# One sum per chunk for two parts of the output projections

## The chip, the cores and the metric

The kernel runs on one core of a Trainium2 chip: TensorE (PE) for matmuls, VectorE (DVE), ScalarE (ACT) and GpSimd (POOL) for the elementwise work, and SyncE (SP) for issuing DMAs. The metric is the device time of one execution in microseconds, as the median of some runs.

## What is computed

A decoder trunk of two layers on one sequence of 512 tokens with 1024 channels, in float32. Cut to what matters here:

```
for each layer:
    h = rms_norm(x)
    heads = attention(h @ w_in)        # 16 heads of 64; layer 0: 8 dilated, 8 sliding-window; layer 1: 16 forgetting
    x = x + concat(heads) @ w_out      # the output projection, 1024 x 1024
    h = rms_norm(x)
    x = x + relu(h @ w_up)**2 @ w_down
```

The output projection with its residual, `x + concat(heads) @ w_out`, is what the change is about.

## The kernel before

**Products in three parts.** Every operand of a large matmul is kept as a high half rounded to fp32r and the low half that remains (`split`, `parts`). `mm3` makes three matmuls of 128 x 128 weights and 512 columns: high weights with high data, low with high, high with low. A weight tile is loaded raw (tag `wraw`, 4 buffers, which the residual's tiles `xl` and the MLP's weights share), then split into `whi` and `wlo` (7 buffers each). Which engine does the two halves goes by a table: `PAT_OP` for the output projection.

**Pairs of heads.** Heads are worked in pairs of 64 rows each, eight pairs per layer. `attend` makes a head's scores (`S`, then the reduction `negm`, the exponential, the sum `den` and its reciprocal `rden`), scales the probabilities `P`, transposes them (`PT`) and multiplies them with the values (`O`). While one head's scores are made, the values of the head before run. With a pair's second head `yf` is complete and is split into `y`.

**The output projection.** `out_part(pairs, first, ...)` makes the part of the product that belongs to some pairs: for each of eight chunks of 128 output channels it sums `mm3` over these pairs in one PSUM bank `op` and adds the bank to the accumulator `acc` on VectorE. The first part adds the residual `xl`; the later ones add to what `acc` holds. There are three parts: in layer 0 pairs 0, 1, 4, 5, then 6, 7, and in the end 2, 3; in layer 1 pairs 0 to 3, then 4, 5, and in the end 6, 7. The last part belongs to the MLP's function, which takes up each chunk at once (`finish`), and whose weights `w_up` are loaded ahead.

**What sets the order.** `run` interleaves the attention of the last pairs with the first two parts of the output projection: it takes a step of one or of the other by their shares of the work (`LEADS`). A scheduler then orders each engine's instructions, except those that are kept in program order. PSUM has eight banks here: four (`pA`) for `pj` and `op`, four (`pB`) for the attention's `S`, `PT`, `O` and `qkT`. SP issues its DMAs in order: weights, the residual, and the copies of K to the other half of the partitions (line 313).

Of the kernel before, what the change touches and what calls it, by code (L numbers as in the profile page):

```python
# [9 lines left out]
F32 = mybir.dt.float32  # L10
# [8 lines left out]
P = 128  # L19
# [10 lines left out]
RAW = 4  # L30
# [15 lines left out]
REST = 11  # L46
UNP = True
AHEAD = ()
LD1 = 6
PRE0 = 3  # L50
LS = 2
# [9 lines left out]
LEADS = (0.0, 0.0, -0.16, 0.33, -0.3, -0.23, -0.09)  # L61
# [8 lines left out]
def trunk(ctx, tc, x, b_sinks, w_out_even, b_forget, w_out_odd, w_up, w_down, xt, gains, w_in_even, w_in_odd, out):  # L70
    nc = tc.nc
# [5 lines left out]
    wp = ctx.enter_context(tc.tile_pool(name="wp", bufs=3))  # L77
# [3 lines left out]
    def bank(tag, name):  # L81
        return ps.tile([P, 512], F32, tag=tag, bufs=BANKS[tag], name=name)
# [4 lines left out]
    def acc_slot(name):  # L87
        return act.tile([P, 2, 512], F32, tag="acc", bufs=4, name=name)
# [74 lines left out]
    def mm3(o, wh, wl, xh, xl, start, stop, pin=False, more=False):  # L163

        m = nc.tensor.matmul(o, wh, xh, start=start, stop=False, skip_group_check=more)  # L165
        if pin:
            tc.keep_in_program_order(m)
        nc.tensor.matmul(o, wl, xh, start=False, stop=False, skip_group_check=more)  # L168
        nc.tensor.matmul(o, wh, xl, start=False, stop=stop, skip_group_check=more)  # L169
# [23 lines left out]
    def residual(li, dp):  # L193

        return xsp[dp] if li else xt[dp * 256:(dp + 1) * 256].rearrange("(c p) t -> p c t", p=P)

    def layer_attention(li, hT, w_in, w_out, stats=None):


        with ExitStack() as c2:  # L200
# [211 lines left out]
            ys = [None] * 8  # L412
# [31 lines left out]
            def last_values():  # L444
                for _ in head_values(last_head[0]):
                    yield
                last_head[0] = None

            def chain(*gens):
                for g in gens:  # L450
                    yield from g

            def run(att, n_att, dense, n_dense, lead=0.0):

                a = d = 0
                while True:
                    if d / n_dense <= (a + lead * n_att) / n_att or att is None:
                        c = next(dense, None)
                        if c is None:
                            break  # L460
                        d += c
                    else:
                        if next(att, "end") == "end":
                            att = None
                        a += 1
                if att is not None:
                    for _ in att:
                        pass

            accs = []  # L470

            def out_weights(pairs, c0):

                np_ = len(pairs)
                w = 1024 // np_
                runs, k = [], 0
                while k < np_:
                    m = k
                    while m + 1 < np_ and pairs[m + 1] == pairs[m] + 1:
                        m += 1  # L480
                    runs.append((k, 0, w_out[pairs[k] * P:(pairs[m] + 1) * P, c0 * P:c0 * P + w]))
                    k = m + 1
                return load_w(runs, w, np_, PAT_OP)

            def out_part(pairs, first, finish=None, tiles=None):

                np_ = len(pairs)
                w = 1024 // np_
                tiles = tiles or {}
                for c in range(DC):  # L490
                    c0, e = c // (w // P) * (w // P), c % (w // P)
                    if c0 not in tiles:
                        tiles[c0] = out_weights(pairs, c0)
                    ws = tiles[c0]
                    cw = slice(e * P, (e + 1) * P)
                    if first and c % 2 == 0:
                        xl = wp.tile([P, 2, 512], F32, tag="wraw", bufs=RAW, name="xl")
                        nc.sync.dma_start(xl, residual(li, c // 2))
                        accs.append(acc_slot(f"acc{li}_{c // 2}"))
                    o = bank("pA", "op")  # L500
                    for kk, n in enumerate(pairs):
                        mm3(o, ws[kk][0][:, cw], ws[kk][1][:, cw], ys[n][:, 0], ys[n][:, 1], kk == 0, kk == np_ - 1)
                    a = accs[c // 2][:, c % 2]
                    nc.vector.tensor_add(a, o, xl[:, c % 2] if first else a)
                    if finish is not None:
                        finish(c, a)
                    yield 32 * np_

            tiles = {}

            def ahead(pairs):
                for c0 in AHEAD:
                    tiles[c0] = out_weights(pairs, c0)
                    yield 0
# [18 lines left out]
            def all_of(gen):  # L533
                for _ in gen:
                    pass

            if li == 0:
                def qk_a(g):
                    return project([(g * 768, g * 768 + 512)], qk_use(g, 8))

                def v_a(g):
                    return project([(g * 768 + 512, g * 768 + 768)], v_use(g, 0), PAT_START if g == 0 else PAT_ATT)

                def att_a(g):
                    def get(p_):
                        qk = st["qk", g]
                        return prep_q(qk, p_ * P), prep_k(qk, 256 + p_ * P, gg[:, 0:1])
                    return attend(get, 256, lambda: st["v", g], lambda j: j, "a", 4 * g, 2, 2 * g)

                def kv_b():  # L550
                    def use(outs):
                        st["v", 3] = prep_v(outs, P, 2, 1)
                        st["k", "b"] = norm_heads(outs, 2)
                    return project([(2048, 2304)], use, PAT_START)

                def att_b():
                    def get(p_):
                        if p_ == 0:
                            st["kb"] = prep_k(st["k", "b"], 0, gg[:, 1:2])
                        k = st["kb"][p_ // 2]  # L560
                        return prep_q(st["qk", "b"], p_ * P), [k, k]
                    return attend(get, 0, lambda: st["v", 3], lambda j: j // 4, "b", 0, 4, 4)

                start(ap, hT, w_in, make_tables(ap, dist, lt, lb), [bank("pA", f"pj{t}") for t in range(NT)], qk_use(0, 8, "P3", 2))
                all_of(v_a(0))
                run(att_a(0), 32, chain(kv_b(), project([(1536, 2048)], qk_use("b", 8))), 768, LEADS[0])
                run(att_b(), NB, chain(qk_a(1), v_a(1)), 768, LEADS[1])
                run(chain(att_a(1), last_values()), 38, chain(out_part([0, 1, 4, 5], True),
                                                              out_part([6, 7], False), ahead([2, 3])), 1536, LEADS[2])
                last = [2, 3]  # L570
            else:
                def qk_c(g):
                    return project([(g * 768, g * 768 + 512)], qk_use(g, 8))

                def v_c(g):
                    return project([(g * 768 + 512, g * 768 + 768)], v_use(g, g))

                def vf_c():
                    def use(outs):
                        forget(ap, outs)  # L580
                        v_use(0, 0)(outs)
                    return project([(512, 768), (3072, 3088)], use, PAT_START)

                def att_c(g):
                    def get(p_):
                        qk = st["qk", g]
                        return prep_q(qk, p_ * P), prep_k(qk, 256 + p_ * P, gg[:, 2:3])
                    return attend(get, 256, lambda: st["v", g], lambda j: j, "c", 4 * g, 2, 2 * g)

                g = vf_c()  # L590
                for _ in range(STATS):
                    next(g)
                stats()
                all_of(g)
                all_of(qk_c(0))
                for g in range(3):
                    run(att_c(g), 36, chain(qk_c(g + 1), v_c(g + 1)), 768, LEADS[3 + g])
                run(chain(att_c(3), last_values()), 42, chain(out_part([0, 1, 2, 3], True),
                                                              out_part([4, 5], False), ahead([6, 7])), 1536, LEADS[6])
                last = [6, 7]  # L600

            def finish(f):
                all_of(out_part(last, False, f, tiles))

            return accs, finish

# [635 lines left out]
    accs, end = layer_attention(0, [], w_in_even[0], w_out_even[0])  # L1242
    hT, stats = mlp(0, accs, end, False)
    accs, end = layer_attention(1, hT, w_in_odd[0], w_out_odd[0], stats)
# [39 lines left out]
```

## Time and profile before

| | us |
|---|---|
| median of 3 runs | 1161.94 |
| lowest, highest | 1161.77, 1162.87 |
| the profiled execution | 1160.99 |
| its span | 1159.2 |

The granted TensorE clock is 1.00 of full speed over the whole span. PE is the matmul engine and PEld its weight loads, which overlap the matmuls. In a timeline a matmul's end is modelled, and matmuls overlap each other; a distance of two starts says when the engine took the next. Rows of one line and shape that follow each other are put together, with their count behind. What stands in brackets is the idle time ahead of an instruction and what ended it. An instruction that waits holds up all that stands behind it on its engine or queue.

### The profile page before, as it was taken

The page shows a single profiled execution, that of the slowest core. Times are in us where ns is not written, and L with a number is a line of the kernel's source. Part 1 is how long each engine was busy: PE and PEld are TensorE (multiplying, and loading weights), DVE is VectorE, ACT ScalarE, POOL GpSimd, SP SyncE. Part 2 cuts the span into 40 slices and gives each one's busy share as a digit, 9 for nine tenths or more (in the row PEclk, how much of TensorE's full clock was granted, in tenths as well). Part 3 has the DMA queues.
Part 4 walks back from the last instruction along what each step waited for, and adds up shares of the span by engine and source line. Part 5 has one row for each costly group of instructions (what it writes and reads, how often), then busy time and mean ns, then how long its engine had stood idle before and what let it go on. Part 6 is the DMA issues. An engine that isn't in the chain of part 4 may idle for free.

```text
span 1159.2 us, 17365 instructions
## 1 busy us (share of the span) xinstructions
PE 1141.9 (99%) x6228; PEld 977.8 (84%) x6228; DVE 873.0 (75%) x1865; ACT 645.2 (56%) x1342; POOL 198.1 (17%) x292
## 2 busy tenths in 40 slices
PE   9999999999999999999999999999999999999998
PEld 7887887888989988988988888888888888888887
DVE  7878899969868857855647877778858759669676
ACT  7555867655545455444335685655756455465452
POOL 0445434100000000000255545332100000000000
PEclk9999999999999999999999999999999999999999
DMA  8432114232333332433443433343420722523403
GB/s 288 131 91 74 55 38 146 75 108 91 93 108 92 112 105 76 123 96 111 147 128 109 110 101 98 111 129 117 161 86 18 230 80 67 188 73 111 147 34 109
DMA packets 94695, 126.57 MB, mean 109 GB/s; under 512 B 5888, under 2 KB 66304, under 8 KB 94608
## 3 DMA queue, kind: packets, MB, share of 16 engines
q1 hardware_dynamic: 93568, 123.29, 34.7%
q10 hardware_dynamic: 1040, 2.16, 0.5%
q8 instruction: 49, 0.80, 0.3%
q14 instruction: 38, 0.31, 0.1%
HBM read 114.39 MB, written 4.23 MB: 102 GB/s over the span
## 4 chain that ended last, share of the span: by engine, by line
PE 84%; DVE 8%; DMA 3%; ACT 2%; issue 2%; POOL 1%; SPq 0%; POOLq 0%; DVEq 0%; ACTq 0%
PE up L165 10%; PE up L169 10%; PE up L168 10%; PE pj L236 4%; PE pj L234 4%; PE pj L235 4%; PE O L405 3%; PE PT L385 2%; PE op L169 2%; PE op L165 2%; PE op L168 2%; PE Y L1045 2%; PE Y L1042 2%; PE Y L1044 2%; PE Y L1091 1%
## 5 line engine op out<-in xcount | busy, mean ns | idle before, releaser
L165 PE MATMUL up<-xin,whi 128*128 128x512 f32 x512 | 200.6, 392 | 0.0
L169 PE MATMUL up<-xin,whi 128*128 128x512 f32 x512 | 199.4, 389 | 0.0
L168 PE MATMUL up<-xin,wlo 128*128 128x512 f32 x512 | 199.3, 389 | 0.0
L791 ACT CAST whi<-wraw 128x512 fp32r<-128x512 f32 x228 | 139.2, 619 | 105.1 <-PE up L169 47.7
L792 DVE TENSOR_TENSOR wlo<-wraw,whi 128x512 fp32r<-128x512 f32 x228 | 151.6, 685 | 50.9 <-ACT whi L791 50.7
L169 PEld LDWEIGHTS up<-xin,whi 128*128 128x128 f32 x512 | 96.1, 188 | 20.1
L168 PEld LDWEIGHTS up<-xin,wlo 128*128 128x128 f32 x512 | 96.2, 188 | 19.9 <-issue 0.2
L165 PEld LDWEIGHTS up<-xin,whi 128*128 128x128 f32 x512 | 96.2, 188 | 19.6 <-issue 0.2
L365 ACT ACTIVATE P<-P,negm 128x128 f32<-128x128 f32 (+5 forms) x128 | 69.5, 543 | 42.7 <-DVE negm L362 40.3
L973 ACT ACTIVATE u<-up 128x512 f32<-128x512 f32 x64 | 38.3, 598 | 90.9 <-PE up L169 90.9
L234 PE MATMUL pj<-whi,hn 128*128 128x512 f32 (+2 forms) x256 | 88.7, 347 | 0.0
L236 PE MATMUL pj<-whi,hn 128*128 128x512 f32 (+2 forms) x256 | 87.0, 340 | 0.0
L235 PE MATMUL pj<-wlo,hn 128*128 128x512 f32 (+2 forms) x256 | 86.9, 339 | 0.0
L153 POOL TENSOR_SCALAR whi<-wraw 128x512 fp32r<-128x512 f32 x88 | 59.7, 680 | 158.7 <-PE pj L236 137.6
L812 DVE TENSOR_TENSOR t<-u 128x256 f32<-128x256 f32 x56 | 23.2, 423 | 62.8 <-ACT u L1116 61.1
L156 POOL TENSOR_TENSOR wlo<-wraw,whi 128x512 fp32r<-128x512 f32 x48 | 63.8, 1332 | 21.4 <-ACT whi L151 18.9
L156 DVE TENSOR_TENSOR wlo<-wraw,whi 128x512 fp32r<-128x512 f32 (+1 forms) x71 | 49.0, 698 | 18.6 <-POOL whi L153 15.1
L373 POOL TENSOR_SCALAR P<-P,rden 128x256 f32<-128x256 f32 (+2 forms) x96 | 48.0, 503 | 82.8 <-DVE rden L368 77.2
L397 ACT CAST PT<-PT 128x256 fp32r<-128x256 f32 (+3 forms) x128 | 48.9, 403 | 20.3 <-PE PT L385 19.4
L362 DVE CUSTOM_DVE_ANT_0 P<-S,bias 128x128 f32<-128x128 f32 (+1 forms) x96 | 45.7, 484 | 17.4 <-PE S L351 11.8
L791 ACT CAST whi<-mraw 128x512 fp32r<-128x512 f32 x64 | 38.8, 620 | 33.1 <-DVE mraw L902 14.4
L385 PE MATMUL PT<-ident,P 128*128 128x128 f32 x296 | 53.4, 276 | 2.4 <-DVE negm L362 1.4
(241 smaller groups left out, 3083.5 us busy)
## 6 DMA issues: line engine op xcount, KB each, us to landing
wraw<-in_w_up SPq DMA_DIRECT2D x64, 512.0 KB, 4.3
wraw<-in_w_down SPq DMA_DIRECT2D x56, 512.0 KB, 3.8
wraw<-in_w_in_odd SPq DMA_DIRECT2D x22, 512.0 KB, 3.8
wraw<-in_w_in_even SPq DMA_DIRECT2D x17, 512.0 KB, 5.0
mraw<-in_w_down SPq DMA_DIRECT2D x16, 512.0 KB, 4.7
K<-K SPq DMA_DIRECT2D x26, 256.0 KB, 2.9
bias<-csp SPq DMA_DIRECT2D x16, 256.0 KB, 3.3
wraw<-in_w_out_odd SPq DMA_DIRECT2D x8, 512.0 KB, 3.7
```

The costliest lines, as they stand in the source:

```text
L153: nc.gpsimd.tensor_scalar(dst_h, src, 1.0, 1.0, op0=OP.mult, op1=OP.mult)
L156: in_order((nc.gpsimd if lo == "pool" else nc.vector).tensor_sub(dst_l, src, dst_h.bitcast(F32)))
L165: m = nc.tensor.matmul(o, wh, xh, start=start, stop=False, skip_group_check=more)
L168: nc.tensor.matmul(o, wl, xh, start=False, stop=False, skip_group_check=more)
L169: nc.tensor.matmul(o, wh, xl, start=False, stop=stop, skip_group_check=more)
L234: nc.tensor.matmul(o, xh, hi[:, :n], start=k == 0, stop=False)
L235: nc.tensor.matmul(o, xh, lo[:, :n], start=False, stop=False)
L236: nc.tensor.matmul(o, xl, hi[:, :n], start=False, stop=k == DC - 1)
L365: nc.scalar.activation(p[:, :ne], p[:, :ne], AF.Exp, scale=-1.0, bias=negm[:, i:i + 1], accum_out=den[:, i:i + 1])
L385: nc.tensor.transpose(pt[:, (i - c) * P:(i - c + 1) * P], pr[i][:, kb * P:(kb + 1) * P], ident)
L791: sca(nc.scalar.copy(dst_h, src))
L792: late.append(lambda: vec(nc.vector.tensor_sub(dst_l, src, dst_h.bitcast(F32))))
```

## The change

Of the three parts of an output projection the first two become one: `out_two(pa, pb)` takes for each chunk a bank, sums the four pairs `pa` into it, leaves it open, sums the two pairs `pb` into it later, and adds the bank and the residual to the accumulator once. `OUT_ORDER` is the order of these steps: "a" and "b" with a chunk's number for the two products, "x" for the load of the residual of two chunks. The sums over `pa` of the first four chunks are made ahead of the first product with `pb`, so that up to four chunks are open in the four banks of `pA`. `out_last` is what is left of `out_part`, for the last part. The number of matmuls is the same; of the adds on VectorE eight per layer are gone.

```diff
--- before.py
+++ after.py
@@ -46,6 +46,8 @@
 REST = 11
 UNP = True
 AHEAD = ()
+OUT_ORDER = (("a", 0), ("a", 1), ("a", 2), ("x", 0), ("a", 3), ("b", 0), ("x", 2), ("b", 1), ("b", 2), ("b", 3), ("a", 4),
+             ("x", 4), ("b", 4), ("a", 5), ("b", 5), ("a", 6), ("x", 6), ("b", 6), ("a", 7), ("b", 7))
 LD1 = 6
 PRE0 = 3
 LS = 2
@@ -482,28 +484,53 @@
                     k = m + 1
                 return load_w(runs, w, np_, PAT_OP)
 
-            def out_part(pairs, first, finish=None, tiles=None):
+            def out_two(pa, pb):
+
+
+                ws, xls, os = {}, {}, {}
+
+                def product(c, pairs, start, stop):
+                    w = 1024 // len(pairs)
+                    c0 = c // (w // P) * (w // P)
+                    if (len(pairs), c0) not in ws:
+                        ws[len(pairs), c0] = out_weights(pairs, c0)
+                    cw = slice((c - c0) * P, (c - c0 + 1) * P)
+                    for kk, n in enumerate(pairs):
+                        hi, lo = ws[len(pairs), c0][kk]
+                        mm3(os[c], hi[:, cw], lo[:, cw], ys[n][:, 0], ys[n][:, 1], start and kk == 0,
+                            stop and kk == len(pairs) - 1)
+
+                for what, c in OUT_ORDER:
+                    if what == "x":
+                        xls[c // 2] = wp.tile([P, 2, 512], F32, tag="wraw", bufs=RAW, name="xl")
+                        nc.sync.dma_start(xls[c // 2], residual(li, c // 2))
+                        accs.append(acc_slot(f"acc{li}_{c // 2}"))
+                        continue
+                    if what == "a":
+                        os[c] = bank("pA", "op")
+                        product(c, pa, True, False)
+                        yield 32 * len(pa)
+                    else:
+                        product(c, pb, False, True)
+                        nc.vector.tensor_add(accs[c // 2][:, c % 2], os[c], xls[c // 2][:, c % 2])
+                        yield 32 * len(pb)
+
+            def out_last(pairs, finish, tiles):
 
                 np_ = len(pairs)
                 w = 1024 // np_
-                tiles = tiles or {}
                 for c in range(DC):
                     c0, e = c // (w // P) * (w // P), c % (w // P)
                     if c0 not in tiles:
                         tiles[c0] = out_weights(pairs, c0)
                     ws = tiles[c0]
                     cw = slice(e * P, (e + 1) * P)
-                    if first and c % 2 == 0:
-                        xl = wp.tile([P, 2, 512], F32, tag="wraw", bufs=RAW, name="xl")
-                        nc.sync.dma_start(xl, residual(li, c // 2))
-                        accs.append(acc_slot(f"acc{li}_{c // 2}"))
                     o = bank("pA", "op")
                     for kk, n in enumerate(pairs):
                         mm3(o, ws[kk][0][:, cw], ws[kk][1][:, cw], ys[n][:, 0], ys[n][:, 1], kk == 0, kk == np_ - 1)
                     a = accs[c // 2][:, c % 2]
-                    nc.vector.tensor_add(a, o, xl[:, c % 2] if first else a)
-                    if finish is not None:
-                        finish(c, a)
+                    nc.vector.tensor_add(a, o, a)
+                    finish(c, a)
                     yield 32 * np_
 
             tiles = {}
@@ -565,8 +592,7 @@
                 all_of(v_a(0))
                 run(att_a(0), 32, chain(kv_b(), project([(1536, 2048)], qk_use("b", 8))), 768, LEADS[0])
                 run(att_b(), NB, chain(qk_a(1), v_a(1)), 768, LEADS[1])
-                run(chain(att_a(1), last_values()), 38, chain(out_part([0, 1, 4, 5], True),
-                                                              out_part([6, 7], False), ahead([2, 3])), 1536, LEADS[2])
+                run(chain(att_a(1), last_values()), 38, chain(out_two([0, 1, 4, 5], [6, 7]), ahead([2, 3])), 1536, LEADS[2])
                 last = [2, 3]
             else:
                 def qk_c(g):
@@ -595,12 +621,11 @@
                 all_of(qk_c(0))
                 for g in range(3):
                     run(att_c(g), 36, chain(qk_c(g + 1), v_c(g + 1)), 768, LEADS[3 + g])
-                run(chain(att_c(3), last_values()), 42, chain(out_part([0, 1, 2, 3], True),
-                                                              out_part([4, 5], False), ahead([6, 7])), 1536, LEADS[6])
+                run(chain(att_c(3), last_values()), 42, chain(out_two([0, 1, 2, 3], [4, 5]), ahead([6, 7])), 1536, LEADS[6])
                 last = [6, 7]
 
             def finish(f):
-                all_of(out_part(last, False, f, tiles))
+                all_of(out_last(last, f, tiles))
 
             return accs, finish
```

Three places at which the instructions stand differently follow. The lines of the changed file are some two higher than before (362 is 364, 156 is 158).

VectorE in layer 0, from the Q and K of the last pair to its first head's first reduction (`ISA P`, which gives `negm`); before:

```order
L161 SCALAR_TENSOR_TENSOR K_2457<-qkT_2452,gg_85,K_2457 64x512
L301 TENSOR_TENSOR Q_2447<-qkT_2442,Q_2447 64x512
L329 SCALAR_TENSOR_TENSOR bias_2597<-dist_100,lt_101 128x512
L161 SCALAR_TENSOR_TENSOR K_2461<-qkT_2452,gg_85,K_2461 64x512
L504 TENSOR_TENSOR acc0_2_2427<-op_2487,xl_2425 128x512
L156 TENSOR_TENSOR wlo_2629<-wraw_2626,whi_2628 128x512
L156 TENSOR_TENSOR wlo_2633<-wraw_2626,whi_2632 128x512
L504 TENSOR_TENSOR acc0_3_2545<-op_2546,xl_2543 128x512
L362 ISA P_2474,negm_2468<-S_2471,bias_2466 128x128
```

and after:

```order
L331 SCALAR_TENSOR_TENSOR bias_2591<-dist_100,lt_101 128x512
L303 TENSOR_TENSOR Q_2429<-qkT_2424,Q_2429 64x512
L163 SCALAR_TENSOR_TENSOR K_2439<-qkT_2434,gg_85,K_2439 64x512
L303 TENSOR_TENSOR Q_2429<-qkT_2424,Q_2429 64x512
L515 TENSOR_TENSOR acc0_0_2373<-op_2279,xl_2371 128x512
L163 SCALAR_TENSOR_TENSOR K_2443<-qkT_2434,gg_85,K_2443 64x512
L515 TENSOR_TENSOR acc0_1_2463<-op_2324,xl_2461 128x512
L515 TENSOR_TENSOR acc0_1_2463<-op_2374,xl_2461 128x512
L364 ISA P_2456,negm_2450<-S_2453,bias_2448 128x128
```

The two low parts `wlo` no longer stand ahead of the reduction; adds of three chunks do, where there were two.

GpSimd in layer 0, at the scaling of one head's probabilities (line 373, after: 375; from 170 us on in the trace); before:

```order
L373 TENSOR_SCALAR P_2194<-P_2194,rden_2190 128x128
L373 TENSOR_SCALAR P_2202<-P_2202,rden_2190 128x256
L153 TENSOR_SCALAR whi_2539<-wraw_2532 128x512
L373 TENSOR_SCALAR P_2216<-P_2216,rden_2190 128x384
L373 TENSOR_SCALAR P_2308<-P_2308,rden_2304 128x128
L156 TENSOR_TENSOR wlo_2536<-wraw_2532,whi_2535 128x512
L373 TENSOR_SCALAR P_2316<-P_2316,rden_2304 128x256
L156 TENSOR_TENSOR wlo_2540<-wraw_2532,whi_2539 128x512
```

and after:

```order
L155 TENSOR_SCALAR whi_2532<-wraw_2525 128x512
L158 TENSOR_TENSOR wlo_2529<-wraw_2525,whi_2528 128x512
L158 TENSOR_TENSOR wlo_2533<-wraw_2525,whi_2532 128x512
L375 TENSOR_SCALAR P_2194<-P_2194,rden_2190 128x128
L375 TENSOR_SCALAR P_2202<-P_2202,rden_2190 128x256
L375 TENSOR_SCALAR P_2216<-P_2216,rden_2190 128x384
L155 TENSOR_SCALAR whi_2573<-wraw_2571 128x512
L155 TENSOR_SCALAR whi_2577<-wraw_2571 128x512
```

The splits (`whi` on line 153, `wlo` on 156) stood between the scalings of a head; now a high half and two low ones stand ahead of them, and the next splits behind.

ScalarE in layer 0, from the exponential of the last head but one to the transposes of the last (`whi` on line 791, after: 816, are casts of `w_up`); before:

```order
L365 ACTIVATE P_2527,den_2469<-P_2527,negm_2468 128x512
L791 CAST whi_2802<-wraw_2798 128x512
L370 ACTIVATE P_2527<-P_2527,rden_2470 128x512
L408 COPY yf_2185<-O_2569 64x512
L791 CAST whi_2805<-wraw_2799 128x512
L791 CAST whi_2808<-wraw_2798 128x512
L151 CAST y0_2_2594<-yf_2185 128x512
L397 CAST PT_2623<-PT_2618 128x512
L365 ACTIVATE P_2605,den_2600<-P_2605,negm_2599 128x128
L365 ACTIVATE P_2613,den_2600<-P_2613,negm_2599 128x256
```

and after:

```order
L367 ACTIVATE P_2519,den_2451<-P_2519,negm_2450 128x512
L372 ACTIVATE P_2519<-P_2519,rden_2452 128x512
L410 COPY yf_2185<-O_2557 64x512
L816 CAST whi_2786<-wraw_2782 128x512
L153 CAST y0_2_2588<-yf_2185 128x512
L367 ACTIVATE P_2599,den_2594<-P_2599,negm_2593 128x128
L816 CAST whi_2789<-wraw_2783 128x512
L816 CAST whi_2792<-wraw_2782 128x512
L399 CAST PT_2630<-PT_2625 128x512
L367 ACTIVATE P_2620,den_2594<-P_2620,negm_2593 128x256
L399 CAST PT_2652<-PT_2648 128x384
```

The casts of w_up stood one by one and two ahead of the last head; now one stands ahead of y0_2's cast, and two between the exponentials of the last head, ahead of its first transposed tile.

## Rows read from the trace of the kernel before

**Rows 1.** The page, busy time, share of the span and instructions of each engine.
```profile
PE 1141.9 (99%) x6228; PEld 977.8 (84%) x6228; DVE 873.0 (75%) x1865; ACT 645.2 (56%) x1342; POOL 198.1 (17%) x292
```

**Rows 2.** Windows: us, busy of PE, PEld, DVE, ACT, POOL, PEclk, DMA, GB/s.
```profile
150.00:216.00 66.00, 62.20 (x349) 52.32 (x348) 59.83 (x155) 41.10 (x106) 25.69 (x36) 1.00 0.33 96
216.00:300.00 84.00, 84.00 (x449) 72.54 (x448) 69.86 (x130) 51.67 (x94) 0.64 (x1) 1.00 0.31 95
745.00:826.00 81.00, 80.79 (x463) 68.51 (x462) 67.61 (x160) 48.71 (x109) 26.22 (x34) 1.00 0.42 133
```

**Rows 3.** Groups by form: line, engine, operation, shapes, count; busy, mean ns; idle before.
```profile
L792 DVE TENSOR_TENSOR wlo<-wraw,whi 128x512 fp32r<-128x512 f32 x228 | 151.6, 685 | 50.9 <-ACT whi L791 50.7
...
L791 ACT CAST whi<-wraw 128x512 fp32r<-128x512 f32 x228 | 139.2, 619 | 105.1 <-PE up L169 47.7 <-PE Y L1095 14.1 <-DVE wlo L792 8.1
...
L504 DVE TENSOR_TENSOR acc<-op,acc 128x512 f32<-128x512 f32 x32 | 21.7, 682 | 2.9 <-PE op L169 2.6
...
L370 ACT ACTIVATE P<-P,rden 128x512 f32<-128x512 f32 x24 | 17.4, 724 | 4.5 <-DVE rden L368 4.4
```

**Rows 4.** TensorE's timeline: start us, us, engine, line, work, count, idle before.
```profile
155.21 0.40 PE L168 MATMUL op<-y,wlo 128*128 128x512 f32 x1
156.84 0.39 PE L348 MATMUL S<-K,Q 128*128 128x256 f32 x1 [1.23 <-DVE yf L409]
...
173.04 0.38 PE L385 MATMUL PT<-ident,P 128*128 128x128 f32 x2
174.27 0.33 PE L385 MATMUL PT<-ident,P 128*128 128x128 f32 x1 [0.85 <-POOL P L373]
...
186.89 0.39 PE L168 MATMUL op<-y,wlo 128*128 128x512 f32 x1
187.12 0.39 PE L169 MATMUL op<-y,whi 128*128 128x512 f32 x1
...
188.61 0.40 PE L165 MATMUL op<-y,whi 128*128 128x512 f32 x1
190.41 0.55 PE L385 MATMUL PT<-ident,P 128*128 128x128 f32 x3 [1.41 <-DVE negm L362]
...
213.89 0.63 PE L168 MATMUL op<-y,wlo 128*128 128x512 f32 x2
214.83 0.74 PE L169 MATMUL op<-y,whi 128*128 128x512 f32 x2 [0.32 <-DVE y L156]
...
763.62 0.39 PE L168 MATMUL op<-y,wlo 128*128 128x512 f32 x1
764.11 0.36 PE L348 MATMUL S<-K,Q 128*128 128x256 f32 x1
...
812.70 0.39 PE L169 MATMUL op<-y,whi 128*128 128x512 f32 x1
```

**Rows 5.** VectorE's timeline in both output stages.
```profile
153.26 2.81 DVE L275 TENSOR_TENSOR qk<-qk,rs 128x512 f32<-128x512 f32 x2
...
187.43 2.12 DVE L156 TENSOR_TENSOR wlo<-wraw,whi 128x512 fp32r<-128x512 f32 x2
...
213.48 1.30 DVE L156 TENSOR_TENSOR y<-yf,y 128x512 fp32r<-128x512 f32 x1
...
811.46 0.69 DVE L156 TENSOR_TENSOR y<-yf,y 128x512 fp32r<-128x512 f32 x1
```

**Rows 6.** GpSimd's timeline in layer 0's output stage.
```profile
170.08 0.37 POOL L373 TENSOR_SCALAR P<-P,rden 128x128 f32<-128x128 f32 x1 [9.23 <-DVE rden L368]
...
172.53 1.13 POOL L153 TENSOR_SCALAR whi<-wraw 128x512 fp32r<-128x512 f32 x1 [1.35 <-DMA wraw<-in_w_out_even]
173.63 0.93 POOL L373 TENSOR_SCALAR P<-P,rden 128x384 f32<-128x384 f32 x2
...
212.93 1.30 POOL L156 TENSOR_TENSOR wlo<-wraw,whi 128x512 fp32r<-128x512 f32 x1 [8.62 <-ACT whi L151]
```

**Rows 7.** SP's timeline of DMA issues in layer 0's output stage.
```profile
184.01 3.30 SPq L313 DMA_DIRECT2D K<-K  x2
```

## The prediction

> **What bounds the kernel now.** I read the page first. TensorE is busy for 1141.9 us of the span, 99%, VectorE for 75% [rows 1]. Then I cut out the stretches that the change touches: the two output stages (about 155 to 222 us in layer 0, 758 to 822 us in layer 1) and what follows the first [rows 2]. The reader is to see three things there. In layer 0's stage TensorE is busy 62.20 of 66.00 us, so only 3.8 us stand idle; in layer 1's 80.79 of 81.00. Behind layer 0's stage it is busy 84.00 of 84.00, so time gained in the stage isn't lost in the next one, whose work starts as soon as it is its turn. And VectorE is busy 59.83 of 66.00 us, so a wait of TensorE is likely one for VectorE.
>
> So the bound is TensorE's own stream of matmuls, in its program order, and a change that leaves their number as it is can only win or add idle time. The next view is TensorE's timeline around each gap [rows 4]. A 512-column output matmul is shown 0.39 long, but the next one starts 0.23 later (186.89 and 187.12), so a stall costs the distance of two starts less 0.23, which is some 0.16 more than the idle column says:
> at 155: 155.21 to 156.84, 1.63 - 0.23 = 1.40;
> at 173: the idle 0.85 and the 0.16, 1.01;
> at 189: 188.61 to 190.41, 1.80 - 0.23 = 1.57;
> at 214: two matmuls from 213.89, the next at 214.83, 0.94 - 0.46 = 0.48;
> in layer 1, at 764: 763.62 to 764.11, 0.49 - 0.23 = 0.26.
> That is 4.46 us in layer 0 and 0.26 in layer 1. Nothing that reorders these stages can win more than 4.72 us there.
>
> **The change part by part.** It takes eight adds per layer off VectorE, those that add a second part to the accumulator. Here 32 adds of this form take 682 ns each [rows 3], of which 16 go: 16 x 0.682 = 10.9 us of VectorE. The matmuls stay, 3 per chunk and pair. As TensorE is the bound, the 10.9 us count only where they stand before something that TensorE waits for. The loads of weights and of the residual change places as well, and so do the splits.
>
> The stall at 155 comes from VectorE's two normalising multiplications, 2.81 us from 153.26 [rows 5], ahead of the output stage. Nothing is changed ahead of it: 0.
>
> The stall at 173 is a wait for a probability tile that GpSimd scales (the releaser named is the scaling on POOL) [rows 4]. GpSimd had stood idle for 9.23 us before 170.08, then waited at a weight split for its DMA, 1.35, and ran it for 1.13, with the scaling queued behind it [rows 6]. In the new order (second list of the change) this split and two low parts stand ahead of the first scaling, in the idle stretch, and the three scalings follow each other. So this wait goes, if the load lands in the idle stretch. What is late next: the four transposes of the first block of keys now stand in a row, and the fourth needs the tile that ScalarE scales, 0.72 [rows 3]; before, matmuls stood in between. Bounds: all of it (-1.01), none (0). I take -0.45, about the middle, as the fourth tile was 0.72 of ScalarE behind the third.
>
> The stall at 189 is the largest. TensorE waited for the reduction of the next head's scores (negm), which on VectorE stood behind a pair of low parts of weights, 2.12 us from 187.43 [rows 5], and two adds (first list of the change). In the new order two adds stand there and no split, and 28 rather than 24 output matmuls stand on TensorE between the transposes of Q and K and the scores: 4 x 0.23 = 0.9 us more cover. 2.12 + 0.9 = 3.0 against 1.57, so it is gone with 1.4 to spare: -1.57. (If the splits come to stand at another place of the same chain, it stays: 0.)
>
> The stall at 214 is the wait for the low half of the last y, on VectorE 1.30 us from 213.48 [rows 5]. After, 16 output matmuls instead of 13 lie between the last O and its reader (+0.69 of cover), but the add of the last chunk stands ahead of yf's add, and it waits for a product whose end is three matmuls behind O. Worked through, y's low half ends 0.1 to 0.7 later: -0.5 to +0.1. I take -0.2.
>
> In layer 1 the 0.26 is a wait for a K (the second head's). There 24 matmuls stand ahead of the scores instead of 23: -0.23 (0 to -0.26).
>
> Layer 1's end has no stall now: y's low half took 0.69 from 811.46 [rows 5], to 812.15, and its first reader started at 812.70 [rows 4]. In the new order 13 matmuls stand ahead of this reader instead of 15: it comes 0.46 earlier, at 812.24. The last chunk's add now stands right ahead of y's low half, in place of one that ran under ScalarE's cast, and GpSimd's low part of the next weights begins at about the same time. In layer 0 such a pair (212.93 on POOL [rows 6], 213.48 on VectorE) shows 1.30 for the subtraction instead of 0.69. So y's low half ends between 812.3 and 812.9: a stall of 0.1 to 0.7. I take +0.4.
>
> The SP queue: the loads of the second part's weights (two 512 KB tiles) and a residual now stand ahead of the copy of K that was issued at 184.01 [rows 7]. They wait for tiles that GpSimd's and VectorE's splits release; these now come earlier (above), and I read some 3 us of slack, so 0. If they came late, K's copy and the scores behind it would be late by the same.
>
> Sum: 0 - 0.45 - 1.57 - 0.2 - 0.23 + 0.4 = -2.05 us. The profiled execution took 1160.99 us with a span of 1159.2, so 1.8 lie around the span; it would be 1158.9. The median of the runs is 0.95 higher, 1161.94, and would be **1159.9**. The bounds of the terms are -3.84 (1158.1) and +0.8 (1162.7).
>
> **The rivals.** What a measurement of this kernel can tell from no change is about 0.2%, 2.3 us: faster is below 1159.6, slower above 1164.3.
>
> Rival A: every stall but the first goes and no new one comes: 1.01 + 1.57 + 0.48 + 0.26 = 3.3, 1158.6. For it: three of four are waits behind VectorE or GpSimd, which get freer. Against it: the last chunk's add on the way to the last y.
>
> Rival A2: VectorE is the bound in layer 0's stage. It is busy 59.83 of 66.00 us (91%), and 8 x 0.682 = 5.5 us of it go. Then the stage gives back all that TensorE idles, 4.5: 1157.4. Against it: the first stall lies ahead of all that is moved, and from 186.89 output matmuls start every 0.23 with nothing between them. The Trainium skill (Perfetto Trace Analysis, Identifying the Most-Contended Engine) says that matmul busy time is a bad measure, matmuls being pipelined, and that the busy share of weight loads is the good one. By that rule the trace would read 52.32 of 66.00, 79%, for TensorE [rows 2], and VectorE, with 91%, would be the most contended engine of the stage; the starts 0.23 apart in [rows 4] speak for a full TensorE, and I go by them.
>
> Rival C: the stalls move and do not go. In place of the 1.57 TensorE waits as long for a split that now stands elsewhere in the chain: 0 in sum, 1161.9.
>
> Rival B, slower: the MLP's first splits are drawn together. ScalarE's casts and VectorE's low parts of w_up (0.619 and 0.685 each [rows 3]) waited for weight tiles that were released chunk by chunk; now two casts stand together, released by the first part's matmuls of chunk 5 (counted from 0), on ScalarE ahead of the casts and exponentials of the last head's blocks (third list of the change). If chunk 5's matmuls end after those are due, the last head's chain is late by up to 2 x 0.619 + 2 x 0.685 = 2.6 us per layer. It decides from the point at which the cast's release comes behind the first exponential of the last head; matmuls of the next chunk cover a part. With both layers: +5.2, less -0.45 - 1.57 - 0.23 = -2.25, about +2.9: 1164.9. With one layer: about 1162.3, which is no change.
>
> **How the numbers follow.** The forecast -2.05 gets 0.42, with a third of it (0.13) below 1159.6; rival A 0.20, A2 0.08, C 0.14, B 0.16. Faster: 0.13 + 0.20 + 0.08 = 0.41. Same: 0.29 + 0.14 = 0.43. Slower: 0.16. The range: it has to hold 0.80; forecast, A and C and half of A2 do: from 1157.4 (A2) to 1163.6 (C, with the bounds +0.8 of the terms and half of what B adds in one layer). Left out are B and half of A2.
>
> **What the profile after would show.** Right: in layer 0's stage no wait of TensorE of over a microsecond for negm, the PT transposes at 173 with about half the idle time, and the first stall as it is. Busy time of VectorE falls by about 10.9 us in all, and TensorE's stays at 1142. In layer 1's end a wait of up to 0.7 for y's low half. Wrong: TensorE waiting in the last head's stretch for ScalarE or VectorE (B), a wait of 1 to 2 us for K at the scores (the SP queue), or a wait for weights (wlo, whi) at the head of a chunk, which none of the rows before shows.

## The result, and the profile after

The changed kernel took 1163.73 us (median of 20 runs, 1163.06 to 1165.47) against 1161.73 for the kernel before (20 runs, 1160.95 to 1163.25): 1.0018 of the time, with a 95% interval of 1.0012 to 1.0025. That is 2.0 us slower: small, but clear of noise, on the other side of the forecast (1159.9) and 0.1 us outside the range. The profiled execution took 1163.06 us with a span of 1161.3.

The busy times of the page answer to [rows 1]:

```profile
PE 1143.7 (98%) x6228; PEld 977.4 (84%) x6228; DVE 866.2 (75%) x1849; ACT 644.7 (56%) x1342; POOL 199.1 (17%) x292
```

VectorE's busy time fell by 6.8 us (873.0 to 866.2), not by the 10.9 of the sixteen adds. Some of what is left takes longer (the bias operations 0.85 us in all, the splits of `y` 0.9); and busy time counts overlapping records once, as those of operations that run back to back are (1.28 for two of 0.69): taken one by one, the operations' times fell by 9.5. The windows of the two output stages answer to [rows 2] (us, then busy of PE, PEld, DVE, ACT and POOL, PEclk, DMA share, GB/s):

```profile
150.00:216.00 66.00, 63.63 (x352) 52.61 (x350) 55.24 (x149) 41.23 (x106) 25.96 (x36) 1.00 0.33 96
...
745.00:826.00 81.00, 79.61 (x458) 67.00 (x457) 63.11 (x148) 46.83 (x106) 27.24 (x34) 1.00 0.43 134
```

In layer 0's stage TensorE stands idle for 2.4 us and no longer 3.8. In layer 1's it was 0.2 and is now 1.4. VectorE is 4.6 and 4.5 us less busy in the two windows, and only one of them got better by it.

The waits of TensorE in both stages, from its timeline (start us, us, engine, line, work, count, the idle time ahead and what ended it); they answer to [rows 4]:

```profile
157.05 0.38 PE L350 MATMUL S<-K,Q 128*128 128x256 f32 x1 [1.24 <-DVE yf L411]
...
169.02 0.33 PE L351 MATMUL S<-K,Q 128*128 128x384 f32 x1
169.81 0.44 PE L387 MATMUL PT<-ident,P 128*128 128x128 f32 x2 [0.46 <-DVE negm L364]
...
188.84 0.47 PE L350 MATMUL S<-K,Q 128*128 128x512 f32 x1
...
210.20 0.39 PE L170 MATMUL op<-y,wlo 128*128 128x512 f32 x1
210.78 0.51 PE L407 MATMUL O<-PT,v 128*128 128x256 f32 x2 [0.19 <-DVE PT L400]
...
215.13 0.40 PE L167 MATMUL op<-y,whi 128*128 128x512 f32 x1
216.12 0.50 PE L171 MATMUL op<-y,whi 128*128 128x512 f32 x1 [0.60 <-DVE y L158]
...
785.63 0.39 PE L171 MATMUL op<-y,whi 128*128 128x512 f32 x1
...
787.08 0.36 PE L350 MATMUL S<-K,Q 128*128 128x256 f32 x1 [1.07 <-DVE acc L515]
...
814.20 0.63 PE L170 MATMUL op<-y,wlo 128*128 128x512 f32 x2
815.08 0.74 PE L171 MATMUL op<-y,whi 128*128 128x512 f32 x2 [0.26 <-DVE y L158]
```

The first wait, 1.24 at 157, is as it was. The one at 173 is gone, and one for negm stands at 169.81. The largest, 1.41 at 190, is gone: the scores behind it start at 188.84 with no idle time (190.76 before). New are a wait of O for PT at 210.78, a longer one for the last y at 216.12 (215.13 to 216.12, 0.99 less 0.23 is 0.76; 0.48 before), one of 1.22 at 787.08 (785.63 to 787.08, 1.45 less 0.23) and one at 815.08 (0.88 less 0.46 is 0.42).

A ledger puts the two traces side by side. At the same matmul of the attention I took its start, less the start of the stage's first output matmul, less 0.228 us for each output matmul issued by then; the table has after minus before. Both programs have the same attention work between, so a step in this column is time lost or won there.

| up to | output matmuls before, after | after minus before, us |
|---|---|---|
| layer 0: scores at 169.57, after 170.16 | 39, 37 | +0.83 |
| scores at 174.35, after 174.28 | 44, 42 | +0.17 |
| scores at 190.76, after 188.84 | 85, 82 | -1.46 |
| next head's scores, 195.51, after 193.23 | 96, 90 | -1.13 |
| last scores, 199.79, after 198.84 | 108, 108 | -1.17 |
| first w_up matmul, 224.30, after 224.21 | 192, 192 | -0.31 |
| layer 1: scores at 764.11, after 764.44 | 23, 24 | -0.23 |
| scores at 775.91, after 775.97 | 48, 48 | -0.27 |
| last pair's scores, 786.96, after 787.08 | 83, 78 | +0.93 |
| last scores, 798.71, after 800.17 | 108, 108 | +1.13 |
| first w_up matmul, 822.45, after 824.51 | 192, 192 | +1.73 |

So the stage of layer 0, first output matmul to first w_up matmul, went from 69.33 to 69.02 us, and that of layer 1 from 63.92 to 65.65: +1.4 in sum. The other 0.6 of the two profiles' 2.1 lies outside the stages (0.2 ahead of the first, 0.4 between the two, part of it a K that landed 0.2 later at 642 us). The order there is the same, and the ten profiles of this case differ by more at these places whatever the kernel: the first output matmul starts between 154.86 and 156.02 us, and from one stage to the next it takes between 534.05 and 534.96. So I take it as scatter.

### The profile page after: what moved, and what is told of

Its sections match the earlier page's. It is cut to its first block, busy times and chain, and to the rows that moved or that the text cites. A ratio compares the mean times of both kernels' runs of the same rounds, so it can differ in the third digit from the quotient of the medians.

```text
span 1161.3 us, 17348 instructions
## 1 busy us (share of the span) xinstructions
PE 1143.7 (98%) x6228; PEld 977.4 (84%) x6228; DVE 866.2 (75%) x1849; ACT 644.7 (56%) x1342; POOL 199.1 (17%) x292
## 4 chain that ended last, share of the span: by engine, by line
PE 85%; DVE 7%; DMA 2%; ACT 2%; issue 2%; POOL 1%; SPq 0%; POOLq 0%; ACTq 0%; DVEq 0%
PE up L167 10%; PE up L171 10%; PE up L170 10%; PE pj L238 4%; PE pj L236 4%; PE pj L237 4%; PE O L407 3%; PE PT L387 2%; PE op L171 2%; PE Y L1070 2%; PE Y L1067 2%; PE Y L1069 2%; PE op L170 2%; PE op L167 2%; PE S L350 2%
## 5 line engine op out<-in xcount | busy, mean ns | idle before, releaser
L236 PE MATMUL pj<-whi,h 128*128 128x256 f32 (+1 forms) x160 | 54.2, 339 | 1.3 <-DVE v L163 0.9
```

Source lines behind the costliest of these rows:

```text
L236: nc.tensor.matmul(o, xh, hi[:, :n], start=k == 0, stop=False)
```

## The experiments

The theory after the first look: in layer 1 the attention's chain to the last pair's K does not come earlier when O comes earlier, since ScalarE stands in between. The rows of ScalarE and of SP in layer 1 of the changed kernel:

```profile
780.61 0.62 ACT L153 CAST whi<-wraw 128x512 fp32r<-128x512 f32 x1 [1.37 <-DMA wraw<-in_w_out_odd]
781.25 0.58 ACT L410 COPY yf<-O 64x512 f32<-64x512 f32 x1
```

```profile
776.85 0.38 SPq L186 DMA_DIRECT2D wraw<-in_w_out_odd  x1
...
784.07 0.47 SPq L315 DMA_DIRECT2D K<-K  x1
```

and ScalarE's in the kernel before:

```profile
780.52 0.62 ACT L151 CAST whi<-wraw 128x512 fp32r<-128x512 f32 x1 [1.14 <-DMA wraw<-in_w_out_odd]
781.16 0.58 ACT L408 COPY yf<-O 64x512 f32<-64x512 f32 x1
```

O's eight matmuls began at 778.22 (779.52 before) and ended by 779.7, but the copy of O into yf stands behind a cast of a weight tile, whose load was issued at 776.85; the cast waited 1.37 us for it and began at 780.61. Before, it began at 780.52 and O was itself 1.3 us later, so it held yf's copy back by little. So yf, Q and K, and K's copy on SP (784.07; 783.98 before), are where they were, and fewer output matmuls lie ahead of the scores: 54 up to the last pair's transposes, where there were 60, and 78 up to the scores, where there were 83 (the table). 5 x 0.23 = 1.15 us, which is the new wait of 1.22 but for 0.1. The bracket at 787.08 names an add of VectorE, but the scores read K. Of the two copies of K from 780 to 788 us (the view of the tile K) the first landed 2.9 us after its issue, at 786.95, and the scores began 0.13 later, as they did before (landed at 786.82, begun at 786.96):

```profile
DMA to landing us min/median/max: 2.9/3.7/4.6
```

The order of steps explains the 54: `run` takes a step of the output projection as long as its share lags; before, all these steps had twelve matmuls, and the fifth brought it to 60; now after four steps of twelve a step of six already satisfies the share.

**Which layer.** One layer at a time has the change.

```diff
- run(chain(att_c(3), last_values()), 42, chain(out_two([0, 1, 2, 3], [4, 5]), ...
+ run(chain(att_c(3), last_values()), 42, chain(out_part([0, 1, 2, 3], True), out_part([4, 5], False), ...
```

> Layer 0 has the one sum per chunk, layer 1 the parts of before. Theory 1 (the loss lies in layer 1, at the second pair's K): by the two traces layer 0's stage, first output matmul to first w_up matmul, goes from 69.33 to 69.02 us, so this kernel is within 0.3% of the one before, -0.3 us, and its layer 1 stage takes 63.9 us again. Theory 2 (the loss is spread, as later loads of w_up delay the MLP): about half of the +2.0 us, +1.0 us, is left here.

> Layer 1 has the one sum per chunk, layer 0 the parts of before. Theory 1: the whole loss, +1.7 us against before; the layer 1 stage 65.6 us instead of 63.9, with a wait of about 1.2 us at the scores of the last pair and 0.4 at the last y. Theory 2: +1.0 us.

Layer 0 alone: 1161.21 us against 1161.31 (1162.86 for layer 1 alone in the same session), ratio 0.9999 (0.9991 to 1.0008). Layer 1 alone: 1.0014 (1.0005 to 1.0022), +1.6 us. Layer 0's stage is 69.08 us in the first and layer 1's 65.19 in the second, with a wait at the same place, 0.81 us long (1.04 less 0.23) where it was 1.22:

```profile
786.50 0.39 PE L171 MATMUL op<-y,whi 128*128 128x512 f32 x1
787.54 0.35 PE L350 MATMUL S<-K,Q 128*128 128x256 f32 x1 [0.66 <-DVE acc L515]
```

The loss lies in layer 1, theory 1; it is not spread. In this second kernel layer 0, with the parts of before, took 69.03 us and not 69.33: its wait at 190 was 1.25 and not 1.57. So layer 0's -0.31 is no more than the scatter of such a stage.

**More matmuls ahead of the last pair.** One number of the lead is changed.

```diff
-LEADS = (0.0, 0.0, -0.16, 0.33, -0.3, -0.23, -0.09)
+LEADS = (0.0, 0.0, -0.16, 0.33, -0.3, -0.23, -0.07)
```

> The changed kernel with the lead of layer 1's output stage at -0.07 instead of -0.09: one more second-part product (six matmuls) is put ahead of the transposes of the last pair, 60 output matmuls as before the change and not 54. Theory 1 (TensorE runs out of output matmuls while the attention chain waits elsewhere): the wait of 1.2 us at the scores goes, the stage falls to 64.4 us, -1.2 us against the changed kernel. Theory 3 (the K copy itself is late, behind the residual's load on SP): the wait stays at 1.2 us, and the time is that of the changed kernel, +2.0 us against before.

1164.59 us, ratio 1.0027 (1.0016 to 1.0037): slower still, by about 1 us against the changed kernel. The expectation failed as to the time. TensorE's waits in layer 1 (start us, us, engine, line, work, idle before), and ScalarE's row ahead of the second:

```profile
788.39 0.36 PE L350 MATMUL S<-K,Q 128*128 128x256 f32 x1 [0.34 <-DMA K<-K]
...
794.13 0.44 PE L407 MATMUL O<-PT,v 128*128 128x384 f32 x1 [0.59 <-ACT PT L399]
795.02 0.57 PE L407 MATMUL O<-PT,v 128*128 128x384 f32 x2 [0.45 <-DVE PT L400]
```

```profile
792.48 0.62 ACT L816 CAST whi<-wraw 128x512 fp32r<-128x512 f32 x1 [1.51 <-DMA wraw<-in_w_up]
```

The wait at the scores did fall, from 1.07 to 0.34 idle, as it should with six more matmuls ahead, and its bracket names the copy of K. But the casts of w_up shifted as well. In the changed kernel the first one stands behind all four exponentials of the last pair's first head (at 792.59); here it stands ahead of two of them and waits 1.51 us for its load, and O waits 0.59 and 0.45 for what stands behind it. This is the mechanism of rival B (casts of w_up that hold the last pair's chain), here released by a DMA and not by matmuls; the changed kernel itself does not show it. By the ledger another 1.1 us is lost at the stage's end, where a cast of output weights now stands ahead of yf's copy, as it does at layer 0's end (below), and the wait for the last y is 0.78:

```profile
814.86 0.62 ACT L153 CAST whi<-wraw 128x512 fp32r<-128x512 f32 x1 [1.89 <-PE op L171]
```

The stage took 67.81 us in the profiled execution, which at 1166.02 us is the slowest of this kernel's eight.

**The cast off ScalarE.** Every high half of output weights is made on GpSimd.

```diff
-PAT_OP = (('pool', 'pool'), ('pool', 'dve'), ('pool', 'dve'), ('act', 'pool'))
+PAT_OP = (('pool', 'pool'), ('pool', 'dve'), ('pool', 'dve'), ('pool', 'pool'))
```

> The changed kernel with every high half of output weights on GpSimd; none is cast on ScalarE, where such a cast stands ahead of yf's copy at two places: layer 1 before the last pair (it waits for its DMA until 780.6 us) and layer 0's end (211.55 us). Theory 1 (this cast holds the attention chain, so that the earlier O is no use): yf's copy begins 1.2 us or more earlier at the first place, the wait at the scores goes, and the end of layer 0 waits 0.4 us instead of 0.95: -1.7 us in sum against the changed kernel. Theory 3 (the copy of K or SP's queue is late): the scores' wait stays, -0.5 us. Against both: GpSimd gets eight casts of about 0.6 us more in its queue ahead of scalings of probabilities.

1161.18 us, ratio 0.9999 (0.9990 to 1.0008): the loss is gone. Its ScalarE, SP and TensorE in layer 1, and TensorE at the last y of layer 0:

```profile
779.96 0.58 ACT L410 COPY yf<-O 64x512 f32<-64x512 f32 x1 [0.51 <-PE O L407]
```

```profile
782.77 0.47 SPq L315 DMA_DIRECT2D K<-K  x1
```

```profile
215.03 0.40 PE L167 MATMUL op<-y,whi 128*128 128x512 f32 x1
215.50 0.50 PE L171 MATMUL op<-y,whi 128*128 128x512 f32 x1
...
785.65 0.39 PE L170 MATMUL op<-y,wlo 128*128 128x512 f32 x1
785.88 0.29 PE L350 MATMUL S<-K,Q 128*128 128x256 f32 x1
```

yf's copy begins at 779.96, K's copy is issued at 782.77 and not at 784.07, and the scores start at 785.88 with no wait, with as few matmuls ahead as in the changed kernel. At layer 0's end the first reader of the low half starts 0.47 behind the matmul ahead of it and not 0.99, so that a wait of 0.24 is left of 0.76. The stages: 68.40 and 64.36 us, 0.6 and 1.3 less than in the changed kernel, 1.9 in sum; the medians say about 2. Theory 1 holds: K's copy is issued earlier as soon as the cast is gone, so SP's queue did not hold it.

**Is it the cast by itself?** The same edit on the kernel before.

> The kernel before with every high half of output weights on GpSimd. Theory 1 (the cast on ScalarE costs only where too few output matmuls cover it): before had six more matmuls ahead of the last pair's K, so nothing waits there: 0 us, within 0.5 us of before, its layer 1 stage 63.9 us. Rival (the cast costs by itself, wherever it stands): -1.5 us, as in the changed kernel.

1161.54 us against 1161.70, ratio 0.9999 (0.9990 to 1.0008); layer 1's stage took 63.57. In the order of before, the cast costs nothing that shows; the rival (1.5 us) is out.

**What the adds were worth.** Each add of the bank and the residual is made twice.

```diff
 nc.vector.tensor_add(accs[c // 2][:, c % 2], os[c], xls[c // 2][:, c % 2])
+nc.vector.tensor_add(accs[c // 2][:, c % 2], os[c], xls[c // 2][:, c % 2])
```

> The changed kernel with each add of a bank and the residual made twice (the second writes the same values again): the sixteen adds that the change took from VectorE are back, in the changed order. Theory 1 (the adds were never on the path that sets the end): 0 to +0.7 us against the changed kernel, so +2.0 to +2.7 against before. Theory V (VectorE limits the output stages, and the change's order costs what its relief gives): up to 16 x 0.68 = 10.9 us more, at least +3 us against the changed kernel.

1164.76 us, ratio 1.0030 (1.0018 to 1.0042) against before: 1.0 to 1.4 us more than the changed kernel (by the medians, by the ratios), which is neither theory's number. By the stages layer 0 lost 1.45 (70.47 us) and layer 1 nothing (65.49). About half of layer 0's loss is where the last pair's O waits for ScalarE's cast of PT (1.62 between these starts, less four matmuls of at most 0.23, leaves 0.7):

```profile
203.55 1.05 PE L407 MATMUL O<-PT,v 128*128 128x512 f32 x4
...
205.17 0.39 PE L407 MATMUL O<-PT,v 128*128 128x256 f32 x1 [0.57 <-ACT PT L399]
```

So sixteen adds, 10.9 us by their durations, are worth a little over 1 us where they now stand, and only in layer 0. TensorE, not VectorE, limits these stages, with VectorE near in one of them.

**GpSimd beside VectorE.** In layer 0 the splits went into GpSimd's idle stretch, as foreseen. The changed kernel's VectorE and GpSimd there, and VectorE's in the kernel before:

```profile
165.16 1.36 DVE L331 SCALAR_TENSOR_TENSOR bias<-dist,lt 128x512 f32<-128x512 f16 x1
166.56 0.76 DVE L163 SCALAR_TENSOR_TENSOR K<-qkT,gg,K 64x512 fp32r<-64x512 f32 x1
167.34 0.88 DVE L331 SCALAR_TENSOR_TENSOR bias<-dist,lt 128x512 f32<-128x512 f16 x1
168.15 1.28 DVE L158 TENSOR_TENSOR wlo<-wraw,whi 128x512 fp32r<-128x512 f32 x2
```

```profile
164.68 2.99 POOL L158 TENSOR_TENSOR wlo<-wraw,whi 128x512 fp32r<-128x512 f32 x2
```

```profile
164.94 0.69 DVE L329 SCALAR_TENSOR_TENSOR bias<-dist,lt 128x512 f32<-128x512 f16 x1
165.67 0.76 DVE L161 SCALAR_TENSOR_TENSOR K<-qkT,gg,K 64x512 fp32r<-64x512 f32 x1
166.46 1.29 DVE L504 TENSOR_TENSOR acc<-op,xl 128x512 f32<-128x512 f32 x2
167.66 0.68 DVE L329 SCALAR_TENSOR_TENSOR bias<-dist,lt 128x512 f32<-128x512 f16 x1
```

The two bias operations, 0.69 and 0.68 before, take 1.36 and 0.88 while GpSimd subtracts; the K between them, which reads one of its operands from PSUM, takes 0.76 as before. In the kernel below GpSimd's low halves of output weights are a fill in place of a subtraction (shortened: the condition that picks them is not shown).

```diff
-split(hi, lo, src, *eng)
+nc.gpsimd.tensor_scalar(hi, src, 1.0, 1.0, op0=OP.mult, op1=OP.mult)   # or nc.scalar.copy(hi, src)
+nc.gpsimd.memset(lo.bitcast(F32), 0.0)
```

> The changed kernel without the low halves of the output weights that GpSimd makes: they are set to zero by a fill, which writes and does not read (left out: their part of the product). Theory 4 (GpSimd's subtractions slow VectorE's operations that run beside them and read two operands from SBUF): in layer 0 the bias of 165 us takes 0.69 again and not 1.36, and the subtraction of the last y 0.69 instead of 1.59 and 1.25; the wait for negm at 170 us goes, those at the last y's fall to 0.3 and 0. Rival (GpSimd's work has no part in it, VectorE is slowed by the transfers in flight): the durations stay.

```profile
164.85 0.69 DVE L335 SCALAR_TENSOR_TENSOR bias<-dist,lt 128x512 f32<-128x512 f16 x1
165.57 0.76 DVE L163 SCALAR_TENSOR_TENSOR K<-qkT,gg,K 64x512 fp32r<-64x512 f32 x1
166.36 0.69 DVE L335 SCALAR_TENSOR_TENSOR bias<-dist,lt 128x512 f32<-128x512 f16 x1
...
216.43 0.69 DVE L158 TENSOR_TENSOR y<-yf,y 128x512 fp32r<-128x512 f32 x1 [0.69 <-ACT y L153]
```

```profile
217.07 0.40 PE L167 MATMUL op<-y,whi 128*128 128x512 f32 x1
217.31 0.39 PE L171 MATMUL op<-y,whi 128*128 128x512 f32 x1
```

```profile
164.35 0.99 POOL L180 MEMSET wlo<- 128x512 f32 x2
```

The first bias runs beside the fill from 164.85 to 165.34 and takes 0.69; the second 0.69; the last y's subtraction 0.69 (1.59 in the changed kernel). Theory 4 holds for the durations. The waits for the last y are gone with them: in layer 0 the first reader of the low half starts 0.24 behind the matmul ahead of it (217.07 to 217.31), in layer 1 the wait of 0.42 is 0 (0.46 for two matmuls, 814.19 to 814.65). For the second bias and for y it isn't separated whether the fill is harmless or only shorter, since no fill ran beside them. The time, 1162.99 us or 1.0012 (1.0002 to 1.0022), says nothing more: the scheduler put 33 output matmuls and not 27 between the transposes of Q and K and the scores at 170 us, and these waited for their K (0.94), so the wait for negm could not be compared. The Trainium skill (SBUF — State Buffer, Who interferes with whom) says that a VectorE instruction with two SBUF inputs contends with a GpSimd instruction that reads SBUF, not with one that only writes it. By that the bias (dist and lt from SBUF) is slowed by the subtraction and not by the fill, and K's operation (one input from PSUM) is not slowed, as the rows show.

**The best of both.** One sum in layer 0 alone, with no cast of output weights on ScalarE.

> One sum per chunk in layer 0 alone, and no cast of output weights on ScalarE. By the stages read so far (layer 0's 68.4 us with no cast, layer 1's 63.9 with the parts of before): -0.7 us against before, 1160.6. Rival (what layer 0's stage wins is given back in the MLP): 0.

1160.32 us against 1161.70, ratio 0.9990 (0.9981 to 0.9999): faster than both kernels, by 1.4 us against before (0.7 was expected), just clear of no change. Its stages are 68.35 and 63.47 us, 1.4 less in sum than before.

## Why the prediction was wrong

The frame held: TensorE's stream is the bound, its matmuls are as many as before, and the time moves with the sum of its waits. What failed is the list of waits, at three places: the wait for the last pair's K in layer 1, which the sum puts at nothing because I did not look there (measured +1.2 us); the stall at 173 (-0.45 taken, +0.2 measured); and the stall at 214 (-0.2 taken, +0.9 measured).

- **The stall at 155, 0:** right (1.23 and 1.24 idle).
- **The stall at 189, -1.57:** right. The ledger falls by 1.6 there; 0.3 of it is lost again at the next head.
- **The stall at 173, -0.45:** wrong in sign, +0.2. The wait for GpSimd's scaling did go. I costed the splits in GpSimd's idle stretch at nothing, without asking what VectorE did in that stretch: its bias operations took 0.67 and 0.20 longer beside them, two low halves stood behind, and negm came late at 169.81. Two output matmuls fewer stood ahead of it as well (37 for 39 in the table, 0.46 of cover); how the 0.8 lost there splits between the two, no run shows. Rival C's mechanism, at this place. The sign of it was in [rows 5]: the two low halves of 2.12 us at 187.43 ran beside GpSimd's pair of before,

```profile
185.88 2.52 POOL L156 TENSOR_TENSOR wlo<-wraw,whi 128x512 fp32r<-128x512 f32 x2
```

and two take 1.28 where GpSimd does not subtract (168.15, above). I counted with such a pair at layer 1's end and not here.
- **The stall at 214, -0.2:** wrong. From the last scores to the first w_up matmul the ledger rises by 0.9: 0.35 for O (VectorE's copy of PT stood behind a low half of weights that began at 209.69), and the wait for y that I saw shrink grew from 0.48 to 0.95 (0.76 and a 0.19 ahead of it). I named the add ahead of yf's add and not the cast that now stands ahead of yf's copy on ScalarE:

```profile
211.55 0.62 ACT L153 CAST whi<-wraw 128x512 fp32r<-128x512 f32 x1 [1.88 <-PE op L171]
212.20 0.58 ACT L410 COPY yf<-O 64x512 f32<-64x512 f32 x1
...
213.82 0.62 ACT L153 CAST y<-yf 128x512 fp32r<-128x512 f32 x1 [1.04 <-DVE yf L411]
```

```profile
212.38 0.69 DVE L515 TENSOR_TENSOR acc<-op,xl 128x512 f32<-128x512 f32 x1 [1.47 <-PE op L171]
213.11 0.68 DVE L411 TENSOR_TENSOR yf<-O,yf 64x512 f32<-64x512 f32 x1
214.48 1.59 DVE L158 TENSOR_TENSOR y<-yf,y 128x512 fp32r<-128x512 f32 x1 [0.69 <-ACT y L153]
```

The cast waited 1.88 us for a tile that the last products release, so the copy began some 0.6 late (O's last matmul started at 211.35); the last chunk's add (0.69) held yf's add for another 0.3 (from the copy's end at 212.78 to 213.11), and the subtraction took 1.59 beside GpSimd. Without the cast, and with the add behind yf's, 0.24 of the wait is left (215.03 to 215.50, above); without GpSimd's subtraction nothing of the 0.76 is, though the cast stands there (217.07 to 217.31, above). So it took both to make the wait.
- **Layer 1's K at 764, -0.23:** right to the hundredth.
- **Layer 1's end, +0.4:** right (0.42, with 0.1 behind it), and by the slow subtraction that I had expected: 1.25 us beside GpSimd.
- **The SP queue, 0:** right; no scores in layer 0 wait for a K.
- **What was missing:** the +1.2 at the last pair's scores in layer 1. I had counted the matmuls ahead of one pair's scores (24 for 23) and not ahead of the other's, where 54 stand for 60 up to the transposes and 78 for 83 up to the scores, and did not look at what the chain between O and K stands behind. That term alone is a third of the distance of 3.5 us between the forecast and the stages.

The stages moved by +1.4 where -2.05 was the sum. Of the 3.5 between, 1.2 is the missing wait, 0.65 the stall at 173, 1.1 layer 0's end, 0.3 the head behind 189, and the rest lies in layer 1's smaller steps. Rival A2 (VectorE the bound, by the busy share of weight loads) fell with the doubled adds: 10.9 us of VectorE moved the time by a little over 1 us. Of the slower rivals, B was not what happened, though its mechanism showed when the lead was moved.

The 0.4 us by which layer 1's stage with no cast (64.36) is still above that of before is the wait at its last y, which stays (0.48, at 814.13 us). Open is a share of layer 0's pieces under 0.3 us.

Two sums of the prediction do not come out as they are printed: the lower bounds of the terms add up to -3.24 us (1158.7) and not to -3.84, and 1161.9 + 0.8 + half of 2.6 is 1164.0 and not 1163.6. The measured 1163.73 would lie below that end, but by luck: the waits that made it were not those that the range was made for.

## What to carry to other kernels

Where one engine runs full, a reordering is worth what its waits are, and each wait has two sides: what the full engine has left to do, and what the chain it waits for stands behind. Count the cover (here, matmuls) ahead of every wait and of every place that has none now, and follow the chain through each in-order engine: an instruction that waits for a DMA or a buffer, put in front of a short copy, makes an earlier result useless. An idle stretch of GpSimd was not free here, as VectorE was working on operands from SBUF beside it.

## What the runs showed of the hardware

A VectorE operation with both operands in SBUF took 1.36 and 0.88 instead of 0.69 us beside GpSimd's subtraction, the last y's subtraction 1.59 instead of 0.69, and one that reads an operand from PSUM was not slowed (0.76 and 0.76). GpSimd's two subtractions took 2.99 us there, and 2.52 for the pair at 185.88 in the kernel before, beside which two of VectorE's took 2.12 instead of 1.28. The copy of K landed 2.9 us after its issue, and the scores that read it began 0.13 later. VectorE's busy time fell by 6.8 us where 10.9 us of work was taken away, 1.75 of the difference being bias operations and splits of `y` that took longer.
